# Two transformer blocks on one core: one more raw and one more split buffer for the weights, and two lent split parts in the feed-forward networks

## The chip, the cores and the metric

The kernel runs on one core of a Trainium2 chip. The metric is the device time of one execution in microseconds (us). The text speaks of the core's engines by short names: PE is TensorE (matrix products and transposes), ACT is ScalarE, DVE is VectorE, POOL is GpSimd, SP is SyncE, whose queue here issues the loads of the weights.

## What is computed

The reference is two transformer blocks on 256 tokens with 1024 channels, all in float32. Cut to what matters:

```python
# block 1
x1 = layer_norm(ALPHA * x0 + hybrid_mixer(x0))        # mLSTM and sliding-window attention, w_out
x2 = layer_norm(ALPHA * x1 + cross_attention(x1, mem))  # xa_wq, xa_wo, 256 memory tokens
x3 = layer_norm(ALPHA * x2 + conv_ffn(x2))             # ffn_up (2 x 2816), causal conv of 3, gelu * gate, ffn_down
# block 2; shift1 ... gate2 are the six parts of silu(c) @ mod_w + mod_b
h  = rms_norm(x3, g_pre_mix) * (1 + scale1) + shift1
m  = merged(short_conv(h), stick_breaking_attention(h), mamba2(h)) @ w_o   # gated sum of three mixers
x4 = x3 + gate1 * rms_norm(m, g_post_mix)
h2 = rms_norm(x4, g_pre_ffn) * (1 + scale2) + shift2
gt, up = split(h2 @ w_ffn_in)
x5 = x4 + gate2 * rms_norm((silu(gt) * up) @ w_ffn_out, g_post_ffn)
```

ALPHA is 2 ** 0.25. The products with weights are the bulk of the work: each weight is used once, for all 256 tokens.

## The kernel before

**A product.** The activations stand in SBUF with channels on partitions, in two parts: `xh`, rounded to PE's fp32r format, and `xl`, what the rounding left. `hilo` makes such a pair of tiles, from a pool with two buffers for each. The weights are cut into parts of 512 KB (128 partitions x 1024 floats). Each part is split in the same way: ACT writes `wh` (a cast, L194) and DVE writes `wl`, the raw part minus `wh` (L195). A product then is three matrix products, `wh` with `xh`, `wl` with `xh` and `wh` with `xl`: L369, L371 and L373 where the result has channels on partitions (`mmB`), L379, L380 and L381 where it has tokens on partitions (`mmA`).

**The stream of weights.** `weight_order` lists all parts in the order of their use. SP loads them in that order into raw buffers `wst` (L201), of which there are WST = 4; `load` keeps as many in flight. `pump` splits as many parts as there are free split buffers; a split buffer is a pair of tiles, one for `wh` and one for `wl`. There are WSP = 5 of them, and `widen` opens three more from the first mixer to the first part of the second mixer's weights, and again from the boundary x4 to the end. `weights` takes a split part when a product needs it (and splits it then, if it isn't split yet), and `done` gives the buffer back behind the product and pumps again. A raw buffer comes free when DVE has made the low half. Some parts, those of the modulation's weights `mod_w`, are not split: PE uses the raw part (`raw_product`, L320) while it would wait for a norm. `pump` goes no further in the list than such a part as long as it is not used.

**The order on the engines** is the order in which the program issues the instructions; no scheduler changes it. So each engine takes the instructions in the order of the calls, and what waits holds up all behind it on that engine.

**Boundaries.** Where a norm stands between two products (ln1, ln2, ln3, x4), `boundary` runs the norm's chain of short steps on DVE and ACT for each of the two tiles of 128 tokens. The result is turned by PE to channels on partitions (L466), cast on ACT (L469, `x1h`, `x2h`, ...) and its low part made by DVE (L472). PE does other work meanwhile: raw products, or the first tile of the product behind the boundary.

**The start of a feed-forward network.** `ffn` calls `pump()` first. The first 512 channels of the product up are made with tokens on partitions, by `up_first`: its `product(0)` runs before the boundary has ended for the second token tile, its `product(1)` behind it. Then `act0` copies them out of PSUM and PE turns them (`turn`, L1288). In the first network, `act1_first`, ACT copies (L1293 and L1295, name `up`) and a convolution, gelu and gate follow; in the second, `act2_first`, ACT applies Silu (L1809) and DVE multiplies (L1810). The two parts of the network are then cut into eleven steps j; the products down run two steps behind those up.

Of the kernel before, what the change touches and what calls it, by code (L numbers as in the profile page):

```python
# [16 lines left out]
P = 128  # L17
# [9 lines left out]
# columns of the array of small parameters  # L27
# [7 lines left out]
# rows that are broadcast over the partitions  # L35
# [4 lines left out]
# how many parts of the weights, or steps of what runs beside them, lie between two steps of a chain  # L40
# [19 lines left out]
# buffers of the weights: as loaded, and in two parts  # L60
WST = 4
WSP = 5
# halves of the modulation's rows that the tensor engine makes while it waits for a norm
# [3 lines left out]
# the first mixer's projections, and when its inputs are taken  # L67
# [4 lines left out]
# the second mixer's  # L72
# [8 lines left out]
def weight_order():  # L81
    # ("raw", i): a part of the modulation's weights, used as it is
# [42 lines left out]
def block_pair(ctx, tc, a, out):  # L125
# [31 lines left out]
    # the other four banks, one by one or in pairs  # L157
# [20 lines left out]
    class Wide:  # L178
        # 1024 columns in two banks
# [12 lines left out]
    # x in two parts of half the bits each, whose sum is x  # L192
# [32 lines left out]
    # the loaded part goes to use, and the next is loaded  # L225
# [6 lines left out]
    def pump(most=99):  # L232
        while at["part"] < len(order) and most > 0:
# [6 lines left out]
            if base_used[0] < WSP:  # L240
                pool, tag, bufs = wp, "w", WSP
                base_used[0] += 1
            elif more["pool"] is not None and more["used"] < more["n"] and at["split"] < more["until"]:
                pool, tag, bufs = more["pool"], "wx", more["n"]
                more["used"] += 1
            else:
                break
            homes.append(tag)
            h = pool.tile([P, 1024], F32R, tag=tag + "h", name=nm("wh"), bufs=bufs)
            l = pool.tile([P, 1024], F32R, tag=tag + "l", name=nm("wl"), bufs=bufs)  # L250
# [33 lines left out]

    def widen(n, until):
        more["pool"], more["stack"] = opened(nm("wx"), side="right")
        more["n"], more["until"] = n, until
# [14 lines left out]
    def done(n=1, go=True):  # L302
        for _ in range(n):
            if homes[at["done"]] == "w":
                base_used[0] -= 1
            else:
                more["used"] -= 1
            at["done"] += 1
# [3 lines left out]
    # rows of the modulation for 512 columns, by the tensor engine: c over all columns, times the weights  # L312
# [23 lines left out]
    # lets the chains end  # L336
# [10 lines left out]
    # n steps of a chain at a time  # L347
# [14 lines left out]
    # channels on partitions: out[c, t] = sum_k w[k, c] x[k, t]  # L362
# [12 lines left out]
    # tokens on partitions: out[t, c] += sum_k x[k, t] w[k, c], for one k and 512 channels  # L375
# [10 lines left out]
    # a part of the weights, taken at its first use  # L386
# [10 lines left out]
    # the last k of a product with tokens on partitions: one token tile, and one half, after the other; mid after each  # L397
    # part of the weights
# [19 lines left out]
    # a projection with tokens on partitions, a unit of work at each step  # L418
# [35 lines left out]
    def hilo(name="x"):  # L454
        return (ap_.tile([P, KT, S], F32R, tag="xh", name=nm(name + "h")),
                ap_.tile([P, KT, S], F32R, tag="xl", name=nm(name + "l")))

    # src [tokens of tile tt, 1024] -> channels on partitions, in two parts
# [16 lines left out]
    # after a product with tokens on partitions: a chain of short steps on each token tile, whose results (src) become  # L475
    # the channels x. The chain of the second tile goes on between the steps of the first's; fill has what the tensor
    # engine does in the meantime.
# [32 lines left out]
    # scale / sqrt(y) for y > 0: a first guess from the bits of y, and two steps towards the root  # L510
# [45 lines left out]
    # x_new = layer_norm(ALPHA x + acc)  # L556
# [23 lines left out]
    # dst = x gain, and 1 / sqrt(mean(x^2) + eps) over 1024 columns; src gives a half of x  # L580
# [14 lines left out]
    # softplus(x) = max(x, 0) + log1p(exp(-|x|)), by the series of atanh; e = exp(-|x|)  # L595
# [20 lines left out]
    # causal convolutions over the tokens of channels on partitions  # L616
# [29 lines left out]
    # triu[s, t] = 1 where s <= t; the second half is all ones; strict[s, t] = 1 where s < t  # L646
# [5 lines left out]
    # maskp[s, t] = 0 where s <= t, else BIG; maskn = -maskp  # L652
# [3 lines left out]
    # and strictn[s, t] = 0 where s < t, else -BIG  # L656
# [6 lines left out]
    # the inputs, and their two parts, in four pieces  # L663
# [11 lines left out]
    # the first part of the weights comes in two halves, so that work begins early  # L675
# [15 lines left out]
    # ---- work beside the projections: after each half of a part of the weights, every chain goes a step further, and  # L691
    # what a step needs was issued some steps before ----
# [4 lines left out]
    # banks of psB that the chains hold  # L697
# [7 lines left out]
    # takes n of the four banks; the work that frees earlier ones goes first  # L705
# [18 lines left out]
    # stages that follow one after the other; the stage `last` is the last one to read the banks  # L724
# [38 lines left out]
    # mLSTM: decays of the gates  # L763
    def gate_steps():
        yield from need("g")
        # and silu(c) of the second block
# [39 lines left out]
    # window attention of two heads (j0 and j0 + 1) of one kv head  # L806
# [65 lines left out]
    # two blocks of 128 columns of the heads' outputs -> channels on partitions, in two parts  # L872
# [17 lines left out]
    # mLSTM: all pairs of tokens at once, for one head  # L890
# [35 lines left out]
    # norms of two heads, gated  # L926
# [29 lines left out]
    # relative position bias over a band of distances: band[h, u], distance u - 128, and the bias backwards  # L956
# [36 lines left out]
    # gates, values of the window attention, and a part of the output gates  # L993
# [28 lines left out]
    # mLSTM: queries and keys, twice their silu  # L1022
# [77 lines left out]
    # the other keys of the memory fill the wait for the first norm  # L1100
# [85 lines left out]
    # the first 512 channels of a product, with tokens on partitions: one token tile after the other  # L1186
# [36 lines left out]
    def ffn(w_up, w_down, xx, up0, act0, act, hook, after, before=lambda: None):  # L1223
# [60 lines left out]
    # the first 512 channels: token tiles of the product -> channels on partitions  # L1284
# [22 lines left out]
    mods, rows_of = {}, {}  # L1307

    # rows for half of a part, from their sums over all partitions; scales go with the gains of the norms
# [24 lines left out]
    # the same by the vector engine, beside other work  # L1334
# [41 lines left out]
    # steps for the halves from h0 to h1  # L1376
# [5 lines left out]
    # n steps spread over the points of a network, from its step j0 to its step j1  # L1382
# [53 lines left out]
    ffn("ffn_up", "ffn_down", xb, up1, act1_first, act1, hook1, after3, lambda: drain(fill3, LAG["ln3.pre"]))  # L1436
# [504 lines left out]
```

## Time and profile before

| | |
|---|---|
| device time, median of 3 runs | 873.84 us (873.21 to 874.56) |
| span of the profiled execution | 877.4 us |
| PE busy | 851.8 us, 97% |
| PE's weight loads busy | 764.1 us, 87% |
| DVE busy | 626.1 us, 71% |
| ACT busy | 426.0 us, 49% |
| POOL busy | 33.8 us, 4% |
| moved by DMA | 175.02 MB, 199 GB/s on average |

The profiled execution has no other time of its own than its span, which lies 3.6 us above the median of the runs. How to read the profile: busy times are sums over the span, and they overlap between engines. A list of waits names, for each line, what released it and how long the engine had been idle. A timeline row gives the start, the time from the first start to the last end of a group of like instructions, and in brackets the idle time of the engine ahead of them and what ended it. A chain of waits is followed back from the last instruction. The granted clock (PEclk) is a share of PE's full clock of 2.4 GHz; its lower level is 1.2 GHz, and a number between 0.5 and 1 is a stretch with both.

### The profile page before, as it was taken

To read this page: it belongs to the slowest core of one execution; us is meant where nothing else is said; L and a number is where in the kernel's file an instruction comes from. 1 tells how busy PE (TensorE), PEld (TensorE's weight loads), DVE (VectorE), ACT (ScalarE), POOL (GpSimd) and SP (SyncE) were. 2 spreads that over 40 slices of the span, in tenths; PEclk is the share of its full clock that TensorE was granted. 3 is DMA by queue.
4 is the path that set the end of the run, shared out by engine and by line. 5 is a ranking of instruction groups with operands and counts; after the bars stand their busy time and mean duration, and the time that the engine had idled before them with its cause. 6 is when DMAs were issued, how large, how long until landed. Compare 5 with 4: busy or idle time off the path is not lost.

```text
span 877.4 us, 14291 instructions
## 1 busy us (share of the span) xinstructions
PE 851.8 (97%) x5616; PEld 764.1 (87%) x5616; DVE 626.1 (71%) x1046; ACT 426.0 (49%) x629; POOL 33.8 (4%) x48
## 2 busy tenths in 40 slices
PE   7999999999999999999989999999999999999996
PEld 5999877898789999899848988999996899999994
DVE  5688678575568997787576889679778775555443
ACT  5555644365356655555236555444354554444431
POOL 2100000000000000000010000002310000000000
PEclk9999999999999999999999999999999999999998
DMA  8954555285277886677277846465675686656611
GB/s 275 310 183 122 166 191 159 107 266 187 79 259 250 280 247 233 191 244 227 83 256 249 311 149 211 147 216 191 218 242 179 220 261 192 203 191 188 180 66 48
DMA packets 49508, 175.02 MB, mean 199 GB/s; under 512 B 5576, under 2 KB 5712, under 8 KB 49440
## 3 DMA queue, kind: packets, MB, share of 16 engines
q1 hardware_dynamic: 46224, 162.76, 57.1%
q0 software_dynamic: 3216, 11.34, 4.2%
q8 instruction: 44, 0.72, 0.3%
q14 instruction: 24, 0.20, 0.1%
HBM read 173.02 MB, written 1.06 MB: 198 GB/s over the span
## 4 chain that ended last, share of the span: by engine, by line
PE 76%; DMA 4%; DVE 2%; ACT 1%; issue 1%; DVEq 0%; ACTq 0%
PE pb L369 14%; PE pb L373 14%; PE pb L371 14%; PE pa L379 8%; PE pa L380 8%; PE pa L381 8%; PE pb L320 3%; DMA wst<-in_w_a 1%; DVE wl L195 1%; PE pb L1139 1%; PE pb L1165 1%; PE pb L1365 1%; DMA wst<-in_mod_w 1%; DMA wst<-in_ffn_up 1%; DMA wst<-in_xa_wq 1%
## 5 line engine op out<-in xcount | busy, mean ns | idle before, releaser
L195 DVE TENSOR_TENSOR wl<-wst,wh 128x1024 fp32r<-128x1024 f32 (+3 forms) x260 | 315.5, 1223 | 165.1 <-ACT wh L194 163.9
L194 ACT CAST wh<-wst 128x1024 fp32r<-128x1024 f32 (+3 forms) x260 | 267.5, 1036 | 279.8 <-PE pb L373 133.8
L379 PE MATMUL pa<-wh,hh 128*128 128x512 f32 x176 | 69.6, 395 | 0.0
L380 PE MATMUL pa<-wl,hh 128*128 128x512 f32 x176 | 69.2, 393 | 0.0
L381 PE MATMUL pa<-wh,hl 128*128 128x512 f32 x176 | 69.0, 392 | 0.0
L369 PE MATMUL pb<-x3h,wh 128*128 128x256 f32 x320 | 53.4, 289 | 0.0
L369 PE MATMUL pb<-x2h,wh 128*128 128x256 f32 x320 | 52.5, 286 | 0.7 <-DVE cv L626 0.7
L369 PE MATMUL pb<-x4h,wh 128*128 128x256 f32 x320 | 51.6, 283 | 0.0
L373 PE MATMUL pb<-x3l,wh 128*128 128x256 f32 x320 | 51.4, 283 | 0.0
L371 PE MATMUL pb<-x3h,wl 128*128 128x256 f32 x320 | 51.4, 283 | 0.0
L373 PE MATMUL pb<-x2l,wh 128*128 128x256 f32 x320 | 51.2, 282 | 0.0
L371 PE MATMUL pb<-x2h,wl 128*128 128x256 f32 x320 | 51.1, 282 | 0.0
L373 PE MATMUL pb<-x4l,wh 128*128 128x256 f32 x320 | 51.1, 282 | 0.0
L371 PE MATMUL pb<-x4h,wl 128*128 128x256 f32 x320 | 51.1, 282 | 0.0
L369 PEld LDWEIGHTS pb<-x2h,wh 128*128 128x128 f32 x320 | 44.4, 190 | 2.8 <-issue 2.1
L626 DVE SCALAR_TENSOR_TENSOR cv<-pb,sm,cv 128x255 f32<-128x255 f32 (+2 forms) x106 | 43.5, 473 | 3.5 <-ACT cv L622 3.5
L369 PEld LDWEIGHTS pb<-x3h,wh 128*128 128x128 f32 x320 | 44.2, 192 | 1.9 <-issue 1.6
L369 PEld LDWEIGHTS pb<-x4h,wh 128*128 128x128 f32 x320 | 44.3, 190 | 1.1 <-issue 0.5
L373 PEld LDWEIGHTS pb<-x3l,wh 128*128 128x128 f32 x320 | 44.1, 192 | 0.0
L371 PEld LDWEIGHTS pb<-x3h,wl 128*128 128x128 f32 x320 | 44.1, 191 | 0.0
L373 PEld LDWEIGHTS pb<-x2l,wh 128*128 128x128 f32 x320 | 43.9, 191 | 0.0
L371 PEld LDWEIGHTS pb<-x2h,wl 128*128 128x128 f32 x320 | 43.8, 190 | 0.0
(429 smaller groups left out, 1626.0 us busy)
## 6 DMA issues: line engine op xcount, KB each, us to landing
wst<-in_ffn_up SPq DMA_DIRECT2D x44, 512.0 KB, 4.5
wst<-in_ffn_in SPq DMA_DIRECT2D x44, 512.0 KB, 3.6
raw<-in_mod_w SPq DMA_DIRECT2D x32, 512.0 KB, 4.4
wst<-in_w_gl SPq DMA_DIRECT2D x24, 512.0 KB, 4.2
wst<-in_ffn_down SPq DMA_DIRECT2D x22, 512.0 KB, 4.2
wst<-in_ffn_out SPq DMA_DIRECT2D x22, 512.0 KB, 3.6
wst<-in_mod_w SPq DMA_DIRECT2D x16, 512.0 KB, 3.6
wst<-in_w_qk SPq DMA_DIRECT2D x12, 512.0 KB, 5.0
```

The costliest lines, as they stand in the source:

```text
L194: A.copy(xh, src)
L195: V.tensor_tensor(xl, src, xh.bitcast(F32), ALU.subtract)
L320: T.matmul(pm_, cs[:, k:k + 1].to_broadcast([P, P]), st[:, e, :], start=(k == 0), stop=(k == KT - 1))
L369: T.matmul(dst, wh[:, k - k0, c0:c0 + P], xh[:, k, t0:t1], start=(k == ks[0]), stop=False)
L371: T.matmul(dst, wl[:, k - k0, c0:c0 + P], xh[:, k, t0:t1], start=False, stop=False)
L373: T.matmul(dst, wh[:, k - k0, c0:c0 + P], xl[:, k, t0:t1], start=False, stop=(k == ks[-1]))
L379: T.matmul(dst[:, c0:c1], xh[:, k, tsl], wh[:, kw, c0:c1], start=first, stop=False)
L380: T.matmul(dst[:, c0:c1], xh[:, k, tsl], wl[:, kw, c0:c1], start=False, stop=False)
L381: T.matmul(dst[:, c0:c1], xl[:, k, tsl], wh[:, kw, c0:c1], start=False, stop=last)
L626: V.scalar_tensor_tensor(dst[:, j:S], ps[:, 0:S - j], taps[K - 1 - j], dst[:, j:S], ALU.mult, ALU.add)
L1139: T.matmul(pl[:, tt * S:(tt + 1) * S], qx[:, 2 * h + e, tt * P:(tt + 1) * P], kx[:, 2 * h + e, :], start=(e == 0), stop=(e == 1))
L1165: T.matmul(pl[:, e * S:(e + 1) * S], vx[:, mt, ct * P:(ct + 1) * P], pT[:, mt, :], start=(mt == 0), stop=(mt == 1))
```

## The change

Three things are deeper. There is one raw buffer more (WST 5) and one split buffer more (WSP 6). And a network gets two split parts more: the two tiles of `hilo` become one tile with both parts, and at its start `ffn` takes such a tile, the one of the pool's two buffers that is free during the network, for two more split parts (`lend`, name `lent`). `pump` uses them when the other split buffers are taken, up to the last part of w2_a in the first network and to the end in the second, and `done` gives them back. The scratch for descriptors of POOL's DMAs is set to 4096, which makes room in SBUF. All other lines of the difference are comments that are left out; by them and by the new lines, line numbers are higher in the changed kernel (L1293 is L1309 there, L469 is L484, L1288 is L1304, L1809 is L1826).

```diff
-WST = 4
-WSP = 5
+WST = 5
+WSP = 6
@@ pump
             elif more["pool"] is not None and more["used"] < more["n"] and at["split"] < more["until"]:
                 pool, tag, bufs = more["pool"], "wx", more["n"]
                 more["used"] += 1
+            elif lent["free"] and at["split"] < lent["until"]:
+                pool = None
             else:
                 break
-            homes.append(tag)
-            h = pool.tile([P, 1024], F32R, tag=tag + "h", name=nm("wh"), bufs=bufs)
-            l = pool.tile([P, 1024], F32R, tag=tag + "l", name=nm("wl"), bufs=bufs)
+            if pool is None:
+                h, l = home = lent["free"].pop(0)
+                homes.append(home)
+            else:
+                homes.append(tag)
+                h = pool.tile([P, 1024], F32R, tag=tag + "h", name=nm("wh"), bufs=bufs)
+                l = pool.tile([P, 1024], F32R, tag=tag + "l", name=nm("wl"), bufs=bufs)
@@ block_pair
+    lent = {"free": [], "until": 0}
+    def lend(until):
+        t = ap_.tile([P, 4, 1024], F32R, tag="xhl", name=nm("lent"))
+        lent["free"], lent["until"] = [(t[:, 0], t[:, 1]), (t[:, 2], t[:, 3])], until
@@ done
-            else:
+            elif homes[at["done"]] == "wx":
                 more["used"] -= 1
+            else:
+                lent["free"].append(homes[at["done"]])
@@ hilo
-        return (ap_.tile([P, KT, S], F32R, tag="xh", name=nm(name + "h")),
-                ap_.tile([P, KT, S], F32R, tag="xl", name=nm(name + "l")))
+        t = ap_.tile([P, 2, KT, S], F32R, tag="xhl", name=nm(name + "hl"))
+        return t[:, 0], t[:, 1]
@@ ffn
-    def ffn(w_up, w_down, xx, up0, act0, act, hook, after, before=lambda: None):
+    def ffn(w_up, w_down, xx, up0, act0, act, hook, after, end, before=lambda: None):
+        lend(end)
         pump()
@@ the calls of ffn: end is
+        first_of["w2_a"] + 8      (first network)
+        len(order)                (second network)
@@ after narrow() behind the first network
+    assert len(lent["free"]) == 2
@@ kernel
-    nc = _bacc.Bacc("TRN2", target_bir_lowering=False, num_devices=1)
+    nc = _bacc.Bacc("TRN2", target_bir_lowering=False, num_devices=1, dynamic_dma_scratch_size=4096)
```

The order of PE's and of POOL's instructions is the same as before. On ACT and DVE only the splits (L194, L195) stand elsewhere, on SP the loads of raw parts. Three places on ACT:

ACT at the start of the first network, before (`x2h` is the cast of the network's input, `wh` a weight part's high half, `wst` a raw part, `up` the copy of the first product):

```order
L469 CAST x2h_2254<-pb_2553 128x4x128
L469 CAST x2h_2254<-pb_2558 128x4x128
L194 CAST wh_2595<-wst_2485 128x1024
L194 CAST wh_2601<-wst_2489 128x1024
L194 CAST wh_2607<-wst_2534 128x1024
L194 CAST wh_2613<-wst_2538 128x1024
L1293 COPY up_2624<-pa_2540 128x512
L1295 COPY up_2625<-pa_2627 128x512
L194 CAST wh_2661<-wst_2599 128x1024
L194 CAST wh_2667<-wst_2605 128x1024
```

and with the change:

```order
L484 CAST x2hl_2257<-pb_2549 128x4x128
L484 CAST x2hl_2257<-pb_2554 128x4x128
L194 CAST wh_2591<-wst_2379 128x1024
L194 CAST wh_2597<-wst_2481 128x1024
L194 CAST wh_2603<-wst_2485 128x1024
L194 CAST wh_2609<-wst_2530 128x1024
L194 CAST wh_2615<-wst_2534 128x1024
L194 CAST lent_2590<-wst_2595 128x1024
L194 CAST lent_2590<-wst_2601 128x1024
L1309 COPY up_2634<-pa_2536 128x512
L1311 COPY up_2635<-pa_2637 128x512
L194 CAST wh_2671<-wst_2607 128x1024
```

Five casts and two more into the lent tile stand ahead of the copies, where there were four. The lent tile's two come from the raw parts `wst_2595` and `wst_2601`, which are loaded after the burst's first low halves.

ACT at the start of the second network, before (the table load and `up` are those of Silu):

```order
L469 CAST x4h_6865<-pb_7147 128x4x128
L469 CAST x4h_6865<-pb_7152 128x4x128
L194 CAST wh_7167<-wst_7057 128x1024
L194 CAST wh_7173<-wst_7118 128x1024
L194 CAST wh_7179<-wst_7122 128x1024
L194 CAST wh_7185<-wst_7126 128x1024
L1809 ACT_TABLE_LOAD
L1809 ACTIVATE up_7196<-pa_7128 128x256
L1809 ACTIVATE up_7197<-pa_7201 128x256
L194 CAST wh_7230<-wst_7171 128x1024
```

and with the change:

```order
L484 CAST x4hl_6841<-pb_7116 128x4x128
L484 CAST x4hl_6841<-pb_7121 128x4x128
L194 CAST wh_7137<-wst_6918 128x1024
L194 CAST wh_7143<-wst_7026 128x1024
L194 CAST wh_7149<-wst_7087 128x1024
L194 CAST wh_7155<-wst_7091 128x1024
L194 CAST wh_7161<-wst_7095 128x1024
L194 CAST lent_7136<-wst_7141 128x1024
L194 CAST lent_7136<-wst_7147 128x1024
L1826 ACT_TABLE_LOAD
L1826 ACTIVATE up_7180<-pa_7097 128x256
L1826 ACTIVATE up_7181<-pa_7185 128x256
```

Here, too, three more casts stand ahead of Silu, two of them into the lent tile.

ACT around the end of the boundary ln1, before (`kx` is the last copy of the memory's keys, `x1h` the input of the cross attention):

```order
L194 CAST wh_1673<-wst_1571 128x1024
L568 ACTIVATE junk_1718,lv_1713<-r_1711,lm_1716 128x512
L568 ACTIVATE junk_1720,lv_1713<-r_1711,lm_1716 128x512
L568 ACTIVATE junk_1762,lv_1750<-r_1748,lm_1759 128x512
L568 ACTIVATE junk_1764,lv_1750<-r_1748,lm_1759 128x512
L1108 COPY kx<-pb_1785 128x512
L1108 COPY kx<-pb_1835 128x512
L469 CAST x1h_1574<-pb_1889 128x4x128
L469 CAST x1h_1574<-pb_1894 128x4x128
L469 CAST x1h_1574<-pb_1903 128x4x128
L469 CAST x1h_1574<-pb_1908 128x4x128
L194 CAST wh_1917<-wst_1606 128x1024
```

and with the change:

```order
L194 CAST wh_1677<-wst_1533 128x1024
L583 ACTIVATE junk_1722,lv_1717<-r_1715,lm_1720 128x512
L583 ACTIVATE junk_1724,lv_1717<-r_1715,lm_1720 128x512
L583 ACTIVATE junk_1766,lv_1754<-r_1752,lm_1763 128x512
L583 ACTIVATE junk_1768,lv_1754<-r_1752,lm_1763 128x512
L1123 COPY kx<-pb_1789 128x512
L1123 COPY kx<-pb_1839 128x512
L484 CAST x1hl_1579<-pb_1893 128x4x128
L484 CAST x1hl_1579<-pb_1898 128x4x128
L484 CAST x1hl_1579<-pb_1907 128x4x128
L484 CAST x1hl_1579<-pb_1912 128x4x128
L194 CAST wh_1921<-wst_1576 128x1024
```

The last part that is split ahead of the boundary is now the first of the cross attention's: `wh_1677` stands ahead of the norm's steps in place of a cast behind `x1h`.

## Rows read from the trace of the kernel before

**Rows 1.** The page, its first part: busy time, share of the span, instructions.
```profile
span 877.4 us, 14291 instructions
PE 851.8 (97%) x5616; PEld 764.1 (87%) x5616; DVE 626.1 (71%) x1046; ACT 426.0 (49%) x629; POOL 33.8 (4%) x48
```
**Rows 2.** What PE waited for: us in total, times, longest.
```profile
PE pa L379 <- ACT wh L194: 2.0, 2, 1.5
PE pa L369 <- ACT wh L194: 1.8, 1, 1.8
PE pa L380 <- DVE wl L195: 1.8, 3, 0.8
PE pb L466 <- DVE h__1129_7030 L1400: 1.7, 1, 1.7
PE pb L369 <- DVE cv L626: 0.7, 1, 0.7
PE pb L1139 <- ACT qx L1175: 0.3, 1, 0.3
```
**Rows 3.** Timeline at ln1's end: start, us, instruction, count [idle before].
```profile
172.66 2.05 ACT L469 CAST x1h<-pb 128x512 fp32r<-128x512 f32 x4
175.71 0.74 PE L369 MATMUL pa<-x1h,wh 128*128 128x256 f32 x4 [1.83 <-ACT wh L194]
176.94 0.33 SPq L201 DMA_DIRECT2D wst<-in_xa_wq  x1
176.97 0.74 PE L371 MATMUL pa<-x1h,wl 128*128 128x256 f32 x4 [0.52 <-DVE wl L195]
```
**Rows 4.** The chain that ended last, loads on it: start (issue), us to landing.
```profile
185.33 4.38 DMA wst<-in_xa_wo
...
254.90 5.40 DMA wst<-in_ffn_up
...
461.20 3.52 DMA wst<-in_w_a
```
**Rows 5.** Timeline of ACT at ln3's end.
```profile
462.67 0.84 ACT L194 CAST wh<-wst 128x776 fp32r<-128x776 f32 x1 [0.58 <-DMA wst<-in_w_a]
464.74 0.84 ACT L194 CAST wh<-wst 128x776 fp32r<-128x776 f32 x1 [1.23 <-DMA wst<-in_w_a]
```
**Rows 6.** Windows: stretch, us, busy PE, PEld, DVE, ACT, POOL; PEclk, DMA share, GB/s.
```profile
176.00:180.00 4.00, 3.48 (x29) 3.27 (x29) 4.00 (x4) 2.50 (x3) 0.00 (x0) 1.00 0.47 145
460.00:464.00 4.00, 4.00 (x18) 3.19 (x18) 3.34 (x4) 2.70 (x4) 0.00 (x0) 0.72 0.77 221
674.00:678.00 4.00, 4.00 (x9) 1.92 (x8) 3.72 (x13) 1.01 (x3) 0.00 (x0) 0.59 0.04 14
```
**Rows 7.** Timeline of DVE ahead of x4's chain (L588 is its next step).
```profile
661.81 2.48 DVE L195 TENSOR_TENSOR wl<-wst,wh 128x1024 fp32r<-128x1024 f32 x2 [0.63 <-ACT wh L194]
```
**Rows 8.** Timeline of the first network's start, SP, ACT and PE.
```profile
252.63 3.73 SPq L201 DMA_DIRECT2D wst<-in_ffn_up  x4
253.72 0.59 ACT L1293 COPY up<-pa 128x512 f32<-128x512 f32 x1
257.42 0.60 PE L1288 MATMUL pb<-ident,up 128*128 128x128 f32 x4
```
**Rows 9.** Timeline of the second network's start, SP, ACT, DVE and PE.
```profile
689.05 3.73 SPq L201 DMA_DIRECT2D wst<-in_ffn_in  x4
690.62 1.28 ACT L1809 ACT_TABLE_LOAD   x1
691.92 0.39 ACT L1809 ACTIVATE up<-pa 128x256 f32<-128x256 f32 x1
692.35 0.41 DVE L1810 TENSOR_TENSOR up<-up,pa 128x256 f32<-128x256 f32 x1
692.91 0.38 PE L1288 MATMUL pb<-ident,up 128*128 128x128 f32 x2
695.31 1.05 ACT L194 CAST wh<-wst 128x1024 fp32r<-128x1024 f32 x1 [0.82 <-DMA wst<-in_ffn_in]
```

More of the change, by code (lines that the diff above doesn't have):

```diff
@@ L305, in done @@
                 base_used[0] -= 1
+            elif homes[at["done"]] == "wx":
+                more["used"] -= 1
             else:
-                more["used"] -= 1
+                lent["free"].append(homes[at["done"]])
             at["done"] += 1
@@ L1434, in after3 @@
         return boundary("ln3", chain, lambda tt: hs_[tt], xb3, fill3, 4 * len(RAW["ln3"]) + 8 - LAG["ln3.pre"])
-    ffn("ffn_up", "ffn_down", xb, up1, act1_first, act1, hook1, after3, lambda: drain(fill3, LAG["ln3.pre"]))
+    ffn("ffn_up", "ffn_down", xb, up1, act1_first, act1, hook1, after3, first_of["w2_a"] + 8, lambda: drain(fill3, LAG["ln3.pre"]))
     xb = xb3
@@ L1827, in hook2 @@
         spread(n_steps(10, 12), 1, NJ - 1, j, point)
-    ffn("ffn2_in", "ffn2_out", xb, up2, act2_first, act2, hook2, lambda acc: lambda tt: after5(tt, acc[tt]))
+    ffn("ffn2_in", "ffn2_out", xb, up2, act2_first, act2, hook2, lambda acc: lambda tt: after5(tt, acc[tt]), len(order))
     narrow()
```

## The prediction

> **What bounds the kernel now.** I began with the page. TensorE (PE) is busy for 851.8 of 877.4 us [rows 1], so the most that deeper buffers can take away is the time in which PE waits for a split part of the weights or for work that queues behind one; where PE is already fed, more buffers buy nothing. The list of PE's waits came next. Six of its lines have to do with splits [rows 2]: waits for a cast or a low half of a weight part (1.8 us under L369, 2.0 under L379, 1.8 under L380), 1.7 us for the scaled rows at the boundary x4, 0.7 for a convolution, 0.3 for a query. The timelines of those places then show what each one ended on, and two more timelines, of the starts of the feed-forward networks, show two places where PE does not wait today and where the order of ACT's instructions changes.
>
> This execution's span is 877.4 us, 3.6 us (0.4%) above the median of the runs shown, 873.84. I make the sum on the span and carry the difference over. A difference under 0.2% (1.75 us) counts as no change, since a measurement of this kernel can't tell it.
>
> **The change part by part: what it takes away.** Every term is read at the place where one more part is now split or loaded ahead of a boundary.
>
> *End of ln1.* PE's first product of the cross attention starts at 175.71, after 1.83 us of idle time that ends on a weight cast which stands on ACT behind the four casts of x1h (172.66, 2.05 us for four); the second group waits another 0.52 for the low half on DVE [rows 3]. With nine split buffers in place of eight this part is split before the boundary. PE then needs only three of the four x1h pieces, at 172.66 + 3/4 x 2.05 = 174.2; its second group can follow 0.5 later, at 174.75 in place of 176.97: **-2.2 us**. Ends: -1.5 (a low half of x1 that comes late) and -2.35 (both idle times).
>
> *The query copy at 190.8.* On ACT it stands behind a cast whose load took 4.38 us [rows 4]. With a raw part more in flight that cast is earlier: **-0.4**, with 0 as the other end (the wait itself is 0.3 [rows 2]).
>
> *The convolution at 270* waits because DVE's instructions stand behind splits of late loads: **-0.8** (0 if they stay late; 0.7 is listed, [rows 2]).
>
> *ln3.* Eight raw parts of the modulation's weights fill the raw buffers, so the eight parts of w2_a are loaded one by one while PE waits. The last but one is cast at 462.67 and the last at 464.74, both straight from a load [rows 5]. With a fifth raw buffer every part is loaded where the one before it was: 464.74 - 462.67 = **-2.1**. Ends: -1.0 (the train of loads is limited by the DMA engines and not by the buffers) and -4.7 (the shift is two parts, and PE's clock stays up: granted clock 0.72 in 460 to 464 [rows 6], (1 - 0.72) x 4 = 1.1 us).
>
> *x4.* Two low halves, 2.48 us, run on DVE right ahead of the chain whose end PE waits for [rows 2, 7]. One of them is now done earlier: half of it, **-0.6** (0 to -1.2). PE's clock was granted at 0.59 in the 4 us behind this wait [rows 6], which costs (1 - 0.59) x 4 = 1.6 us. At the end of ln1 PE was idle for 1.83 and 0.52 us and the clock of the next stretch stayed at 1.00 [rows 3, 6]. So the shortened wait, some 1.1 us, should leave it up: **-1.6** (0 if not).
>
> Together -6.1, and -7.7 with the clock.
>
> The extra split tile costs PE nothing in the steady state: there ACT and DVE have idle time ahead of most splits (PE's list holds no other wait for them). One load more at the very start competes with the input; PE's waits there end on casts of the input that were issued ahead of it, so I take 0, with +0.5 as the other end. The smaller scratch for POOL's DMAs and the joined tile of high and low parts are taken at 0; POOL is never in PE's list, and the tile's two halves were already written in turn.
>
> **The change part by part: what it adds.** Before each network, `pump()` fills all free split buffers at once. Today that is four casts for four loaded raw parts, and the first copy (or Silu) of the network stands right behind them. Now it is five casts from `wst` and two more into the lent tile. Only five raw parts can be loaded, so casts six and seven need raw buffers that come free when DVE has finished the burst's own first and second low halves. The copy of the network's first product stands behind cast seven on ACT, and PE's transposes (L1288) behind that copy.
>
> *First network.* The four loads that follow the burst are issued from 252.63 on, 3.73 us for four, so one every (3.73 - 0.33) / 3 = 1.13 us (a single issue takes 0.33 [rows 3], and the four in the second network have the same 3.73 [rows 8, 9]); the second is issued at 253.76. How long it takes: 5.40 us for the third of this very train [rows 4], 5.13 for the second of the same train in the second network (issued 690.18, cast at 695.31, straight from the load, [rows 9]), at the least 3.52, the shortest on the chain [rows 4]. I take 5.13, the same place in a like train. Cast seven starts at 258.89 and takes 1.05, the copy 0.59 [rows 8]: PE can go on at 260.57, where it goes on at 257.42 today without a wait. **+3.2** (ends +1.6 and +3.4).
>
> *Second network.* The second load lands at 695.31 [rows 9]; then come the cast (1.05), the table load (1.28), Silu (0.39), DVE's product (0.41): 698.4 in place of 692.91. **+5.5** (ends +3.9 with a load of 3.52, +5.8 with one of 5.40).
>
> *PE's clock behind these stalls.* Behind the 1.7 us wait of x4 it fell, which cost 1.6 us; behind the 1.83 us at ln1 it didn't [rows 2, 3, 6]. The second network's stall is three times as long as either: **+1.6**, from 0 to 3.2. The first network's lies between; the two rows disagree and are equally near, so I take half, **+0.8** (0 to 1.6).
>
> Sum: -7.7 + 3.2 + 5.5 + 1.6 + 0.8 = **+3.4 us**; span 880.8, median 877.2, slower by 0.4%.
>
> One rule speaks against the size of these stalls. The Trainium skill, DMA: Bandwidth & Descriptors, section Anatomy of one DMA, gives a transfer a fixed 2.0 us and bytes / 436e3 for the rest. It was fitted on the software path, while these loads go from SP's queue. For 512 KB it makes an estimate of 3.2 us. By it the stalls would be +1.2 and +3.6 us, and the sum -0.5 with the clock terms kept, no change. The trace doesn't agree: 5.13 and 5.40 us in these trains [rows 4, 9], where four loads are in flight together. My sum goes by the rows.
>
> **The rivals.**
>
> *The buffers pay and the bursts cost little (faster).* Place: cast seven. If its load comes 3.5 us after its issue, as the fastest on the chain does, and the clock holds, the stalls are 1.6 + 3.9 = 5.5 against gains of 7.7: -2.2, 871.6 us. With ln3 at its upper end it is -4.8, 869.0. It decides once the stalls with their clock are below 7.7 - 1.75 = 5.95. For it: with one more raw part loaded, the train behind the burst is needed later, so fewer loads may be in flight. Against: they are issued by the same four low halves at the same spacing.
>
> *The bursts cost nothing.* If ACT's copy didn't wait for cast seven, only the gains remained: 866.1 us. This is also what the practice of overlapping loads with compute by more buffers would promise (the Trainium skill, Trainium Kernel Development and Optimization, Best Practices). Against it: ACT works in order in every row here, and the copy stands behind the two casts in its order.
>
> *Half of it (same).* Stalls as priced, but full clock in both networks and after x4: -7.7 + 8.7 = +1.0, 874.8 us; or short stalls with the clock falling as in the forecast: -2.2 + 2.4 = +0.2, 874.0, which is also about where the page's fixed-and-bytes rule ends. For it: ln1's row. Against: x4's row, where a shorter idle time was enough, and the durations in the two trains.
>
> *The change does nothing.* PE is 97% busy, so the added parts are split under cover: 873.8. Against it: the waits of [rows 2 to 5, 7] are behind splits whose place does change.
>
> **How the numbers follow.** Forecast, the stalls outweigh the gains: 0.66. Half of it: 0.10; nothing: 0.04; both within 0.2%. Short stalls: 0.14; no stalls: 0.06; both faster. So faster 0.20, same 0.14, slower 0.66. The forecast's own range is 875.6 to 881.3: at the top both stalls at their upper ends (9.2) with two falls of the clock (3.2), against gains without x4's clock and with ln3 at -1.0 (5.0), +7.4. The whole range reaches down to 868.5, which takes in the short stalls with ln3's best end, and leaves out the 0.06 without stalls and a tail above. **868.5 to 881.3.**
>
> **What would show it.** Right: a wait of some 3 us ahead of L1304 (was L1288) for the copy at L1309 in the first network, and one of 5 to 6 us ahead of it in the second, with casts into `lent` waiting for loads just before; a granted clock near 0.6 in the 4 us behind the second. No wait left at ln1's end, w_a's last cast some 2 us earlier after the boundary, no more than 1.2 us of wait at x4 and a clock of 1.00 there. Wrong: PE starts its transposes right behind the product; or loads that land in 3.5 us; or gains at ln3 and x4 that reach 4 us and more.

## The result, and the profile after

| | before | after |
|---|---|---|
| device time, median of 13 runs each | 877.06 us (872.53 to 880.84) | 879.88 us (877.90 to 887.04) |
| ratio, 95% interval | | 1.0055 (1.0036 to 1.0075) |
| span of the profiled execution | 877.4 us | 877.1 us |

The change is slower by 0.55%. The quotient of the two medians, 1.0032, is smaller, since before's 13 runs lie in two groups, around 874 and around 879 us, and their median falls into the upper one; the quotient of the means (880.88 and 876.44 us) is 1.0051. On the 873.84 us that the prediction started from, 0.55% is +4.8 us (+3.1 to +6.6), 878.7 us. The direction was the one forecast, and the forecast +3.4 lies inside that interval; but as a time, 877.2 us is what the kernel before itself takes over 13 runs, and two of the prediction's steps didn't hold, the one at x4 and the one from a single execution to the median. The two spans are equal because the profiled execution of before was a long one of its kind. A second profile of the same kernel, further down, has a span of 873.0.

What PE waited for, after (us in total, times, longest):

```profile
PE pa L384 <- ACT x0hl L194: 6.3, 2, 5.3
PE pb L1304 <- DVE up L1827: 4.4, 1, 4.4
PE pb L1304 <- ACT up L1309: 2.6, 1, 2.6
PE pa L395 <- DVE wl L195: 2.2, 1, 2.2
PE pb L481 <- DVE h__1097_6999 L1416: 1.7, 1, 1.7
...
PE pa L384 <- ACT x1hl L484: 0.4, 1, 0.4
```

The first line is no new wait: it belongs to the start, and before it was 6.4 us (L369 behind x0h). Set against [rows 2], the waits for the cast of a weight part, for the convolution and for the query are gone, and two new ones stand at L1304, the transposes that begin each network. The wait at x4 (L481) is as long as it was.

The first network's start (timeline of SP, ACT and PE), which answers to [rows 8]:

```profile
246.89 2.60 SPq L201 DMA_DIRECT2D wst<-in_ffn_up  x3
251.80 1.04 ACT L194 CAST lent<-wst 128x1024 fp32r<-128x1024 f32 x1 [2.75 <-DMA wst<-in_ffn_up]
253.02 1.04 ACT L194 CAST lent<-wst 128x1024 fp32r<-128x1024 f32 x1 [0.18 <-DMA wst<-in_ffn_up]
253.97 0.58 ACT L1309 COPY up<-pa 128x512 f32<-128x512 f32 x1
254.60 1.12 PE L1304 MATMUL pb<-ident,up 128*128 128x128 f32 x4 [2.58 <-ACT up L1309]
```

ACT idles 2.75 us ahead of the first cast into the lent tile, since its load was issued only at 246.89, behind the burst's first low half. The copy stands behind the second such cast and PE behind the copy: 2.58 us. PE's four transposes then take 1.12 us where they took 0.60.

The second network's start, which answers to [rows 9]:

```profile
681.81 2.60 SPq L201 DMA_DIRECT2D wst<-in_ffn_in  x3
685.33 1.05 ACT L194 CAST lent<-wst 128x1024 fp32r<-128x1024 f32 x1 [1.02 <-DMA wst<-in_ffn_in]
686.97 1.05 ACT L194 CAST lent<-wst 128x1024 fp32r<-128x1024 f32 x1 [0.58 <-DMA wst<-in_ffn_in]
688.03 1.28 ACT L1826 ACT_TABLE_LOAD   x1
690.22 0.69 PE L1304 MATMUL pb<-ident,up 128*128 128x128 f32 x2 [4.38 <-DVE up L1827]
```

The same chain, longer by the table load, Silu and DVE's product. The windows behind the two waits (columns as in [rows 6]) show the clock:

```profile
254.00:258.00 4.00, 3.40 (x16) 3.40 (x17) 3.31 (x4) 3.89 (x6) 0.00 (x0) 0.57 1.00 367
686.00:690.00 4.00, 0.00 (x0) 0.00 (x0) 3.03 (x4) 3.39 (x6) 0.00 (x0) 0.76 1.02 375
690.00:694.00 4.00, 3.78 (x18) 3.78 (x19) 3.54 (x5) 3.75 (x4) 0.00 (x0) 0.50 0.91 315
694.00:698.00 4.00, 4.00 (x32) 4.00 (x32) 3.96 (x5) 1.06 (x1) 0.00 (x0) 0.89 0.92 296
```

The granted clock is 0.57 in the 4 us behind the first wait, and 0.50 and 0.89 in the 8 us behind the second: (1 - 0.57) x 4 = 1.7 us, and 2.0 + 0.4 = 2.4 us of PE's time.

### The profile page after: what moved, and what is told of

Its sections match the earlier page's. It is cut to its first block, busy times and chain, and to the rows that moved or that the text cites. A ratio compares the mean times of both kernels' runs of the same rounds, so it can differ in the third digit from the quotient of the medians.

```text
span 877.1 us, 14304 instructions
## 1 busy us (share of the span) xinstructions
PE 849.6 (97%) x5616; PEld 766.2 (87%) x5616; DVE 625.7 (71%) x1046; ACT 424.8 (48%) x629; POOL 33.8 (4%) x48
## 4 chain that ended last, share of the span: by engine, by line
PE 79%; DVE 2%; DMA 1%; ACT 1%; issue 1%; DVEq 0%; ACTq 0%
PE pb L384 15%; PE pb L386 15%; PE pb L388 14%; PE pa L395 8%; PE pa L394 8%; PE pa L396 8%; PE pb L335 2%; PE pa L384 1%; PE pa L388 1%; PE pa L386 1%; PE pb L1154 1%; PE pb L1180 1%; PE pb L1381 1%; DMA wst<-in_ffn_up 1%; DVE wl L195 0%
## 5 line engine op out<-in xcount | busy, mean ns | idle before, releaser
L195 DVE TENSOR_TENSOR wl<-wst,wh 128x1024 fp32r<-128x1024 f32 (+3 forms) x236 | 285.4, 1223 | 129.6 <-ACT wh L194 128.0
L194 ACT CAST wh<-wst 128x1024 fp32r<-128x1024 f32 (+3 forms) x236 | 241.6, 1035 | 230.6 <-PE pb L388 125.6
L384 PE MATMUL pb<-x3hl,wh 128*128 128x256 f32 x320 | 53.4, 289 | 0.0
L388 PE MATMUL pb<-x3hl,wh 128*128 128x256 f32 x320 | 51.4, 283 | 0.0
L386 PE MATMUL pb<-x3hl,wl 128*128 128x256 f32 x320 | 51.4, 283 | 0.0
L384 PEld LDWEIGHTS pb<-x3hl,wh 128*128 128x128 f32 x320 | 44.2, 192 | 1.9 <-issue 1.6
L384 PE MATMUL pb<-x2hl,wh 128*128 128x256 f32 x272 | 45.3, 289 | 0.0
L384 PE MATMUL pb<-x4hl,wh 128*128 128x256 f32 x272 | 44.9, 288 | 0.0
L386 PE MATMUL pb<-x4hl,wl 128*128 128x256 f32 x272 | 44.3, 286 | 0.0
L388 PEld LDWEIGHTS pb<-x3hl,wh 128*128 128x128 f32 x320 | 44.1, 192 | 0.0
L386 PEld LDWEIGHTS pb<-x3hl,wl 128*128 128x128 f32 x320 | 44.1, 191 | 0.0
L388 PE MATMUL pb<-x4hl,wh 128*128 128x256 f32 x272 | 43.9, 284 | 0.0
L386 PE MATMUL pb<-x2hl,wl 128*128 128x256 f32 x272 | 43.9, 284 | 0.0
L388 PE MATMUL pb<-x2hl,wh 128*128 128x256 f32 x272 | 43.9, 284 | 0.0
L1373 DVE SCALAR_TENSOR_TENSOR macc<-raw,cs,macc 128x512 f32<-128x512 f32 x56 | 43.0, 767 | 1.1
L195 DVE TENSOR_TENSOR lent<-wst,lent 128x1024 fp32r<-128x1024 f32 x24 | 29.4, 1224 | 15.8 <-ACT lent L194 15.7
L194 ACT CAST lent<-wst 128x1024 fp32r<-128x1024 f32 x24 | 25.2, 1049 | 30.2 <-PE pb L388 12.5
L384 PEld LDWEIGHTS pb<-x2hl,wh 128*128 128x128 f32 x272 | 38.2, 193 | 1.8 <-issue 1.4
```

The lines of the kernel that those rows point to most:

```text
L194: A.copy(xh, src)
L195: V.tensor_tensor(xl, src, xh.bitcast(F32), ALU.subtract)
L384: T.matmul(dst, wh[:, k - k0, c0:c0 + P], xh[:, k, t0:t1], start=(k == ks[0]), stop=False)
L386: T.matmul(dst, wl[:, k - k0, c0:c0 + P], xh[:, k, t0:t1], start=False, stop=False)
L388: T.matmul(dst, wh[:, k - k0, c0:c0 + P], xl[:, k, t0:t1], start=False, stop=(k == ks[-1]))
L1373: V.scalar_tensor_tensor(acc_, st[:, e, :], cs[:, k:k + 1], acc_, ALU.mult, ALU.add)
```

## The experiments

PE has the same matmuls in the same order in all these kernels, 5616 of them, so two profiles can be laid side by side matmul by matmul. A "step" below is by how much the distance between the same matmul in two profiles changes at a place, in us; it holds the wait and the slower clock behind it. All steps are against the second profile of before (the first experiment), and each rests on one profile of each kernel.

**Before once more.** No edit.

> The kernel before, once more. The two profiled executions differ by 3.0 us within the first 20 us, where the change does almost nothing. Theory A: that difference is one between executions, not one of the change: a second profile of the kernel before may have PE's first slow stretch end anywhere from 11 to 18 us, and the time is that of before within 0.3%. Theory B: the earlier fifth load of the changed kernel brings it: then this profile again has slow matmuls up to about 18 us.

Time 1.0022 (0.9999 to 1.0045) of before's, so a kernel set against itself came out 0.2% off; span 873.0 where the first profile had 877.4. Two places make the difference, 3.4 and 1.8 us; 0.4 at the query's copy and 0.3 at ln3 go the other way. One is the start. PE in the first profile, then in this one:

```profile
10.99 1.05 PE L371 MATMUL pa<-x0h,wl 128*128 128x256 f32 x4
17.36 1.05 PE L373 MATMUL pa<-x0l,wh 128*128 128x256 f32 x4
18.21 0.78 PE L369 MATMUL pa<-x0h,wh 128*128 128x256 f32 x4
18.83 0.64 PE L371 MATMUL pa<-x0h,wl 128*128 128x256 f32 x4
```

```profile
8.70 1.05 PE L373 MATMUL pa<-x0l,wh 128*128 128x256 f32 x4
10.98 0.64 PE L371 MATMUL pa<-x0h,wl 128*128 128x256 f32 x4
14.45 0.64 PE L373 MATMUL pa<-x0l,wh 128*128 128x256 f32 x4
```

Four matmuls take 1.05 us up to 18.2 there, and 0.64 from 11.0 on here: 3.4 us over all. The other place is x4. First profile, then this one (windows):

```profile
672.00:676.00 4.00, 2.98 (x10) 1.80 (x11) 3.79 (x11) 1.17 (x2) 0.00 (x0) 0.73 0.43 131
676.00:680.00 4.00, 4.00 (x9) 1.81 (x8) 3.90 (x9) 1.45 (x4) 0.00 (x0) 0.84 0.32 71
```

```profile
669.00:673.00 4.00, 2.70 (x12) 1.68 (x13) 3.79 (x11) 1.17 (x2) 0.00 (x0) 1.00 0.43 131
673.00:677.00 4.00, 4.00 (x11) 1.90 (x10) 3.86 (x10) 1.25 (x3) 0.00 (x0) 1.00 0.54 150
```

The clock fell behind x4's wait in one execution of the kernel and not in the next: (1 - 0.73) x 4 + (1 - 0.84) x 4 = 1.7 us. Theory A holds; neither is an effect of the change. The after profile, too, is through with the slow matmuls early, at 12.3.

Against this profile the change's steps are: start +0.4, ln1 -2.3, the query -0.7, the first network's start **+4.5**, its convolution -1.0, ln3 **-3.2**, x4 0.0, the second network's start **+6.7**, the rest -0.3; together +4.1, within the interval of the ratio.

**Without the lent tile.**

```diff
     def ffn(...):
-        lend(end)
         pump()
```

> The change without the lent tile: five raw and six split buffers, and five casts at the start of each network, all of parts that are loaded. Theory A, the two lent casts that wait for loads cost all of the loss: no wait ahead of the transposes of the first network, at most 0.8 us in the second, and the gains stay (ln1 -2.2, query -0.3, convolution -0.7, ln3 -3.1, x4 -1.9): 7 to 8 us faster than before, ratio 0.991. Theory B, the gains at ln3, x4 and the convolution come from the lent parts: only -2.5, ratio 0.997.

Ratio **0.9950** (0.9926 to 0.9974): 4.4 us faster than before, and 1% faster than the change. Steps: ln1 -2.3, convolution -1.0, ln3 -2.9, first network's start +0.1, second +1.1; the query's copy came late in this execution (+1.0, then -0.5). ACT in the second network:

```profile
676.64 4.85 ACT L194 CAST wh<-wst 128x1024 fp32r<-128x1024 f32 x5
681.50 1.28 ACT L1824 ACT_TABLE_LOAD   x1
```

Five casts in a row without a wait, and the table load at once behind them. The fifth still takes its 1.05 us ahead of Silu, and PE waits 0.8 us there. The gains at ln1, ln3 and the convolution are there, so they don't need the lent tile. The ratio alone doesn't decide, since B's 0.997 lies in its interval and A's 0.991 doesn't; by the places theory A holds, with less than its 7 to 8 us: x4 gives nothing. The waits behind the lent casts are the loss.

**The lent tile later**, behind the first copies, and four parts in the first pump.

```diff
     def ffn(...):
-        lend(end)
-        pump()
+        pump(4)
...
                 act0(up0, hid, later)
+                lend(end)
                 pump()
```

> All of the change, but the first pump of a network takes four parts, and the lent tile is taken only behind the first copies (or Silu). Theory A: no wait ahead of the transposes in either network, all gains kept, about 8 us faster than before, ratio 0.991. Theory B: the casts that wait for loads now hold up what stands on ACT behind them, the convolution of the first step, and PE waits there for 2 us or more: ratio 0.994 to 0.996.

Ratio 1.0014 (0.9992 to 1.0035): theory B, and more of it than expected. In the first network the casts into the lent tile now hold up the convolution (timeline of ACT and PE):

```profile
264.60 1.05 ACT L194 CAST lent<-wst 128x1024 fp32r<-128x1024 f32 x1 [1.48 <-DMA wst<-in_ffn_up]
266.27 1.05 ACT L194 CAST wh<-wst 128x1024 fp32r<-128x1024 f32 x1 [0.61 <-DMA wst<-in_ffn_up]
267.50 1.05 ACT L194 CAST wh<-wst 128x1024 fp32r<-128x1024 f32 x1 [0.18 <-DMA wst<-in_ffn_up]
268.45 1.01 ACT L637 ACTIVATE cv<-pb,sm 128x256 f32<-128x256 f32 x2
272.08 1.20 PE L384 MATMUL pb<-x2hl,wh 128*128 128x256 f32 x4 [4.01 <-DVE cv L641]
```

PE waits 4.01 us and runs at a granted clock of 0.50 in the next 4 us; the step is +5.9. In the second network, which has no convolution, nothing is held up, and nothing is gained either. The wait went to the next instruction behind the casts that PE needed.

**The lent tile alone.**

```diff
-WST = 5
-WSP = 6
+WST = 4
+WSP = 5
```

> The lent tile alone: four raw and five split buffers as before, with the tile of both parts and the smaller scratch. At the start of a network four casts are of loaded parts and two wait for loads, the same two loads as in the change. Theory A: both waits are there in full (about 2.6 to 3.2 us and 4.4 to 5.5 us, and a lower clock behind each), and none of the gains at ln1, ln3 and x4: 10 to 11 us slower than before, ratio 1.012. Theory B, the waits come from the fifth raw buffer's loads crowding the queue: less than 3 us slower.

Ratio 1.0111 (1.0072 to 1.0149). Waits of 3.1 and 5.1 us at L1304, steps +4.8 and +7.6. Theory A: the loss comes with the lent tile, without the fifth raw buffer. One gain of the change is here, too, which the expectation didn't have: the convolution's wait is gone (step -1.0).

**No lent tile, four parts in the first pump.**

```diff
     def ffn(...):
-        lend(end)
-        pump()
+        pump(4)
```

> The change without the lent tile (as in the run without it), and the first pump of a network takes four parts; the fifth is split behind the first copies or Silu. Theory: the 0.8 us wait that five casts left at the second network's start goes too, nothing new comes, so 0.8 us faster than the kernel without the lent tile, 5 to 8 us faster than before: ratio 0.994. Rival: the fifth part, split later, is late for the first step's products, and the time is that of the kernel without the lent tile or more (0.995 to 0.997).

Ratio 0.9951 (0.9927 to 0.9976). The second network's 0.8 us wait is gone, and a wait of 0.6 at the convolution is back. In time this kernel and the one with five casts can't be told apart.

**One raw buffer alone.** `WST = 5`, `WSP = 5`, no `lend`.

> One raw buffer more alone: five raw, five split buffers, no lent tile. Theory A, the raw buffer pays at ln3, where split buffers are not short: PE's waits between 447 and 465 us lose some 3 us, the cast behind x1h at ln1's end stays with its waits of 1.8 and 0.5 us: 3 to 4 us faster than before, ratio 0.996. Theory B, the split buffer is needed too: no difference.

Ratio 0.9962 (0.9936 to 0.9989). Steps: ln3 -3.3, convolution -1.0, query -0.9; ln1 0.0, where the waits of 1.8 and 0.5 stay. Theory A. ln3's gain is the raw buffer's, even if the clock, which stayed at 1.00 there in this profile, has a part in its size: the last of w_a's eight parts lands 9.3 us behind the first product with w_a, as against 12.0 in the second profile of before and 9.7 with the change.

**One split buffer alone.** `WST = 4`, `WSP = 6`, no `lend`.

> One split buffer more alone: four raw, six split buffers, no lent tile. The fifth cast at a network's start then is of a part that is still being loaded. Theory A: ln1's end gains 2.2 us, ln3 nothing, and the fifth cast, which waits for the first load behind the burst, holds up the copy (about 1 us in the first network) and Silu (2 to 3 us in the second): 0 to 2 us slower than before, ratio 1.001. Theory B, only the lent parts stall: 2 us faster, ratio 0.998.

Ratio **1.0091** (1.0064 to 1.0118), more than theory A had. ln1 gains its 2.3. But a fifth cast at each burst is of a part that is still on its way; second network, ACT:

```profile
684.38 3.91 ACT L194 CAST wh<-wst 128x1024 fp32r<-128x1024 f32 x4
690.12 1.05 ACT L194 CAST wh<-wst 128x1024 fp32r<-128x1024 f32 x1 [1.84 <-DMA wst<-in_ffn_in]
691.19 1.28 ACT L1824 ACT_TABLE_LOAD   x1
```

Steps +1.5 and +4.4 at the two networks, and one that theory A hadn't: +3.7 at the query's copy, which also stands behind such a cast (PE's wait 2.7). Two smaller ones, -1.0 at ln3 and +1.0 behind it (a wait of 0.9 at L1380), cancel. So a part that is split on top of the raw parts that lie loaded stalls ACT, whatever buffer it goes to.

**The lent tile from the third step of a network on.**

```diff
     def ffn(...):
-        lend(end)
-        pump()
+        pump(4)
...
         for j in range(NJ):
+            if j == 2:
+                lend(end)
```

> All of the change, but the first pump of a network takes four parts and the lent tile is taken at the third step of the network, when PE is fed from split parts and raw parts lie loaded. Theory: the lent parts are harmless there and useless, since PE waits for no split part inside the networks: no new wait, the time of the kernel without the lent tile, ratio 0.995. Rival A, two parts split further ahead pay at ln3: 1 us or more faster than that, ratio 0.993 or less. Rival B, they still hold up a convolution by a microsecond or more: ratio 0.997 or more.

Ratio 0.9971 (0.9946 to 0.9995). The two casts into the lent tile don't wait here (278.79, 2.00 us for both), but they use up two loaded raw parts, a cast behind them waits 2.73 us for its load, and PE waits 1.08 us for a convolution behind that cast (at 295.00). Another wait for a convolution, 1.18 us at 270.13, comes ahead of the lent tile; it was 0.6 in the run without the tile. ln3 gains 2.5, no more than without it (2.8). Rival B, though its interval takes in the theory's 0.995.

**Seven raw buffers, five split buffers**, no lent tile, four parts in the first pump.

```diff
-WST = 5
-WSP = 6
+WST = 7
+WSP = 5
```

> Seven raw buffers and five split buffers, no lent tile, four parts in the first pump of a network: as much room as the change takes outside the lent tile. Theory A, raw buffers are what ln3 lacks (four raw parts gave way to five for 3.3 us): three more let w_a's parts land two or more places earlier: PE's remaining waits there (some 2.5 to 3 us) go to about 1, ln1's end keeps its 2.3 us: 5 to 6 us faster than before, ratio 0.994. Theory B, at ln3 the loads are limited by the DMA engines by then: the same 3.3 us as with five, ratio 0.996.

Ratio **0.9930** (0.9908 to 0.9951), the fastest here: 6.1 us faster than before in the same room. ACT at ln3:

```profile
445.92 3.81 ACT L194 CAST wh<-wst 128x776 fp32r<-128x776 f32 x5
454.07 1.77 ACT L194 CAST wh<-wst 128x776 fp32r<-128x776 f32 x2 [4.34 <-DMA wst<-in_w_a]
```

Five of w_a's parts are cast in a row; the step at ln3 is -4.9. One wait of 2.4 us is left, for the first low half. That isn't late for want of a load, since ACT had cast its part by 446.74. It stands on DVE directly behind the last step of the norm's chain:

```profile
448.20 1.41 DVE L1415 SCALAR_TENSOR_TENSOR h__755_4654<-h__755_4654,rr,mod 128x512 f32<-128x512 f32 x2
449.53 4.47 DVE L195 TENSOR_TENSOR wl<-wst,wh 128x776 fp32r<-128x776 f32 x5
```

So a further raw buffer wouldn't shorten it. ACT itself idles 4.34 us for later loads, but PE doesn't wait for those. Theory A, except that the last wait didn't shrink to 1 us, and that ln1's end (which the expectation wrongly credits) needs a split buffer and stays. How much of the -4.9 is the buffers' is open: the granted clock stayed at 1.00 in this profile's ln3, while in both profiles of before it fell there, at a price of 1.7 us (the first of them has 0.72 in [rows 6]).

**The joined tile and the smaller scratch alone.** `WST = 4`, `WSP = 5`, no `lend`.

> The joined tile of both parts and the smaller scratch alone: four raw and five split buffers, no lent tile. Theory: nothing, ratio 1.000 within 0.003, and all of PE's waits as before. Rival: the joined tile makes a part wait for the other, some 0.5 us at each boundary, ratio 1.002 and new waits for x1, x2, x3 or x4.

Ratio 1.0002 (0.9981 to 1.0024). Nothing, as taken, and no new wait at a boundary. Single steps of this profile are not zero all the same: +1.1 at ln1, where the wait is the old 1.82 us and the clock behind it was granted at 0.64, and -0.9 at the query's copy.

## Why the prediction was right or wrong

**What failed.** The step at x4: "One of them is now done earlier" was to give -0.6 us, and -1.6 more for the clock; the runs showed 0.0. And the step that makes the sum on one execution's span and carries the difference over to the median of three runs: over 13 runs the kernel before takes 877.06 us and not 873.84, and the change 879.88, where 877.2 was forecast. The mechanism that was to decide, casts that wait for loads ahead of what PE needs, was right.

**The stalls.** Right in kind and place. First network +3.2 and +0.8 forecast, +4.5 as a step: the wait 2.6 and 1.7 for the clock. Second: +5.5 and +1.6 forecast, +6.7: the wait 4.4 and 2.4 for the clock. Both waits were shorter than forecast. In the second network the reason is the second load, which took less than the 5.13 us taken from the train of before. It was issued 1.13 us behind the first: 682.94 to 686.97 is 4.0 us. In the first network it took 5.0 us (248.02 to 253.02), nearly as forecast. There the burst stood earlier: its first load was issued 5.1 us ahead of the end of PE's product, and 4.8 in before. (And 258.89 + 1.05 + 0.59 is 260.53, so the forecast should have read +3.1.) The Trainium skill, DMA: Bandwidth & Descriptors, section Anatomy of one DMA, has a rule, fitted on the software path, that makes an estimate of 3.2 us for this size. The trace stays above it in both networks. Both clocks fell, where I had taken half of a fall for the first.

**ln1 and the query.** -2.2 and -0.4 forecast, -2.3 and -0.7. The query's isn't shown to come from a buffer: the two profiles of before differ by 0.4 there, and the kernel with the old buffers and the joined tile has -0.9. At ln1 PE's first product now waits only for x1's high part:

```profile
171.22 0.75 PE L384 MATMUL pa<-x1hl,wh 128*128 128x256 f32 x4 [0.40 <-ACT x1hl L484]
```

**The convolution.** -0.8 forecast, -1.0 measured.

**ln3: too small.** -2.1 forecast, -3.2 measured (-2.9 against the first profile), inside the bounds. The step "every part is loaded where the one before it was" was sized by the last cast alone, and for that it was right: behind the first product with w_a the change gains 2.2 us. The other 1.0 comes ahead of that product, where waits of 0.2 for a raw part and 0.5 for the first cast are gone. The clock has no part in it: it fell at ln3 in these profiles of before and after alike, at a price of 1.7 us each. Now four casts run in a row at the end:

```profile
456.17 3.73 ACT L194 CAST wh<-wst 128x776 fp32r<-128x776 f32 x4 [0.71 <-DMA wst<-in_w_a]
```

PE has one wait left (2.2), where it had five for casts and low halves. As with seven raw buffers, this one is for the first low half behind the norm's chain on DVE.

**x4: wrong.** "One of them is now done earlier: -0.6" and the clock's -1.6 both failed; the wait is 1.7 as before. The chain ahead of it doesn't start from DVE's splits (ACT and DVE):

```profile
656.45 0.69 DVE L603 TENSOR_TENSOR x<-pa,mod 128x512 f32<-128x512 f32 x1 [0.94 <-ACT junk L602]
658.48 0.60 ACT L602 ACTIVATE junk<-pa 128x512 f32<-128x512 f32 x1 [2.06 <-PE pa L396]
659.20 0.69 DVE L603 TENSOR_TENSOR x<-pa,mod 128x512 f32<-128x512 f32 x1 [2.06 <-ACT junk L602]
```

With the split out of the way DVE idles 2.06 us for ACT's square sum, which reads PE's own product. The low halves of [rows 7] ended about when the product did, so taking one away freed nothing. And the clock's fall at x4 was a matter of the execution that was profiled: it fell in one of the twelve profiles here. Against that one the change seems to gain 1.8 us there; against the second, nothing. That the clock read 1.00 behind this wait, as forecast, is luck, since the wait that was to leave it up had not become shorter. Nor is the row at ln1 firm that the forecast leaned on: a wait of the same 1.8 us was followed by a clock of 1.00 in before, and by 0.59 with the lent tile alone and 0.64 with the joined tile alone.

**The sum.** Of the 2.2 us that x4 didn't give, ln3 gave 1.1 back. That leaves +4.5 by the prediction's own terms, near the +4.1 of the profiles and the +4.8 of the runs. That +3.4 came near these is in part luck, as errors on both sides cancelled. The other failed step is to "carry the difference over" from one execution's span to a median of three. Of before's two groups of runs the first three all fell in the lower one, while the span of 877.4 held 3.4 us of a long start and 1.7 us of the clock at x4 that the second profile doesn't have. So against that very profile the change comes out at -0.3 us, with ln3 and x4 at -4.7 together, one of the forecast's own signs of being wrong.

**The rivals.** That the bursts cost nothing, or little, is refuted by the run without the lent tile, 1% faster than the change. The kernels with more raw buffers alone, 0.4% and 0.7% faster than before, show that part of the change's gains was real and that the rest of it spent them.

## What to carry to other kernels

On an engine that works in order, as ACT does in every row here, a prefetch buffer is only as good as the data that lies ready for it. A split buffer without a loaded part puts a wait for a load into the queue of ACT, ahead of whatever stands behind it; so ask of each instruction behind a burst of prefetches who waits for it, and fill only as many buffers as parts lie loaded. Deepen the buffer nearest the memory first: here one raw buffer alone gained 0.4%, and one split buffer alone lost 0.9%. Seven raw and five split buffers gained the most, 0.7%, but that interval overlaps with those of five raw buffers (0.4%) and of five raw and six split ones (0.5%). The lent tile with so many raw buffers that its parts would lie loaded was not tried.

Take a second profile of the kernel before: a term that is there in one execution and not in the next, like a clock's fall, is no gain to forecast.

## What the hardware showed that was not expected

PE's first matmuls run at about half pace until a time that differs between executions of the same kernel, 18.2 and 11.0 us in the two profiles of before. The column of the granted clock reads 1.00 there, so only the matmuls' durations show it. First profile (windows):

```profile
14.00:18.00 4.00, 4.00 (x15) 2.65 (x14) 3.00 (x3) 1.79 (x3) 0.00 (x0) 1.00 0.85 257
```

It is worth 3.4 us. Against the second profile, the start is longer by 3.4 to 4.6 us in four of the other eleven profiles, and lies between -0.4 and +1.4 in seven. That would make two groups of run times like those seen, but this isn't shown. Why it comes early or late wasn't tried.

Behind waits of like length the clock fell in some profiles and stayed at 1.00 in others. Behind 1.6 to 1.7 us at x4 it fell in one of twelve. Behind 1.8 us at ln1 it fell in two of the six that have this wait. At ln3 it fell in six of the twelve: behind the wait for w_a's first low half it fell to 0.57 in the 4 us after 2.2 us in the changed kernel, and stayed at 1.00 after 2.4 us with seven raw buffers. The waits of 2.6 and 4.4 us ahead of L1304 in the changed kernel, and the one of 4.0 us at the convolution, were followed by a clock of 0.50 to 0.57.
